# Seven products of halves in eight couples of the up product, and another order of the last token blocks

## The chip, the cores and the metric

The kernel runs on one core of a Trainium2 chip. The metric is device time in microseconds (us) of one execution; lower is better. A core has TensorE (PE in the profile; PEld is its weight load), VectorE (DVE), ScalarE (ACT), GpSimd (POOL) and SyncE (SP, which here only issues loads). Matmuls write to PSUM, eight banks of 128 x 512 float32; DVE and ACT read PSUM, POOL does not. All data are float32.

## The reference

One encoder layer over 512 tokens of width 1024:

```python
h = _rmsnorm(x, g_pre_mix)
q, k, v, g, u, sv, a_ret, a_sgu = jnp.split(h @ w_in, ...)
y_ret = _retention_branch(q, k, v, g, ret_decay_logit, w_ret_o)
y_sgu = _sgu_branch(u, sv, sgu_ln_g, sgu_ln_b, w_spatial, b_spatial, w_sgu_o)
merged = sigmoid(a_ret) * y_ret + sigmoid(a_sgu) * y_sgu
x = x + _rmsnorm(merged @ w_out, g_post_mix)
h2 = _rmsnorm(x, g_pre_ffn)
hid = h2 @ w_up                      # 1024 -> 2 * 2816
hid = conv over 3 neighbouring tokens, per channel, + conv_b
a, b = jnp.split(hid, 2, axis=-1)
x = x + _rmsnorm((gelu(a) * b) @ w_down, g_post_ffn)
```

The change concerns `h2 @ w_up` and the last few microseconds after `@ w_down`.

## The kernel before

Every matrix product is made in three matmuls: each operand is split into a high part (`hi`, rounded to the matmul's type by an ACT copy) and a low part (`lo = src - hi`, by DVE), and hi·hi, hi·lo and lo·hi are accumulated (`split` L80 to L82; `copy` L75 is the ACT copy). Activations are split once, weights as they arrive.

Weights come as 146 blocks of 128 x 1024 in the order of their use (`wall`). The list `units` (L88 to L107) says what each block becomes: `("blk", i)` is a block split whole (`w_block`); a pair of blocks can also become seven forms, `B11, B21, T1, T2, T3, T4, B22` (`w_form`, L143): the four quarters and their sums T1 to T4, each of 512 columns with its own ACT copy and DVE low. T1 and T3 are DVE adds (L154, L155), T2 and T4 POOL adds (L156, L158). `w_get` hands out the next unit and emits the loads and splits of the units ahead of it, up to nine half-size slots (`w4`); raw blocks have four buffers.

Products of seven: a two-by-two block product is made from seven products of halves in place of eight (Strassen's scheme in Winograd's form). The class `Pair` (L637) does it for two output tiles: `part1` makes four products, `part2` one, `part3` two; each product is 4 k-steps x 3 matmuls of 256 columns (L651), in three PSUM banks, with combinations on DVE and ACT between them. For this it needs sums of activation halves, S1 to S4, that `x_forms` (L280) makes on DVE with ACT copies. The u product (4 Pairs) and the two gate products (8 Pairs, each with two whole blocks `f_block` between its parts, L744 to L752) use it already. The down product uses a scheme of seven too, in its own functions.

The up product does not. Its 44 output tiles of 128 channels (`NF` = 22 tiles i, each with an a and a b half) are `f_block` calls (L626): 8 k-steps x 3 matmuls of 512 columns (L203 to L205). The first four of the 44 are made in two token halves by `early` (L874) while the norm before is still being finished. Loop L948: for each tile the two results go through `conv` (an ACT activation L906, then two DVE operations that read PSUM, L909 and L913), `gated` (ACT gelu, DVE product into `gp`, L922), and after every second tile, for seven pairs, `down_forms` (L929), which prepares the forms of `gp` for the down product: five DVE operations of 256 columns, three lows of 512, and four ACT copies.

At the end (L1067), after the second half of the down product, each of the four token blocks t has its last matmuls (`add_whole`, L993) into two banks: M2 and M3 for t = 0 and 1, M4 and M8 for t = 2 and 3. DVE adds them up (`z`, L1076), ACT sums the squares, POOL takes the power (L815), DVE scales and adds x1 (L1084), and SP and ACT queues write the output.

Order: the code's order is the priority. A planner places every instruction in its engine's queue at build time, the earliest ready one in program order first, by its own estimates; each queue then runs in that fixed order, and waits by semaphores. A PSUM bank is guarded as a whole: a matmul into one half waits for a read of the other half that stands before it.

Of the kernel before, what the change touches and what calls it, by code (L numbers as in the profile page):

```python
# [33 lines left out]
DP = 9  # L34
WHOLE = NF - 2 * DP
EAGER = 7

PRE, FFNG, LNG, LNB = 0, 8, 16, 24
CW, CB = 32, 32 + 3 * 2 * NF
# [4 lines left out]
def tile_block(ctx: ExitStack, tc, xT, x, wall, par, cs, decay, wsp, bsp, gpost, gffn, out):  # L44
# [11 lines left out]
    def blk(dt=F32, n="blk", shape=(P, S)):  # L56
        return sb.tile(list(shape), dt, tag="blk", bufs=NBLK, name=nm(n))

    def tmp(n="tmp", shape=(P, S)):
        return sb.tile(list(shape), F32, tag="tmp", bufs=6, name=nm(n))  # L60
# [24 lines left out]

    RES1 = NW - 22 - 44
    RES0 = RES1 - RES_OUT
    units = []  # L88
    i = 0
    while i < NW:  # L90
        pair = [(f, i) for f in ("B11", "B21", "T1", "T2", "T3", "T4", "B22")]
        if U0 <= i < GATE0:
            units += pair
            i += 2
        elif GATE0 <= i < GATE1:
            units += pair[:4] + [("blk", i + 2)] + pair[4:] + [("blk", i + 3)]
            i += 4
        elif i == DOWN0:
            for _ in range(2):
                pairs = [[("q", i + j), ("t", i + j)] for j in range(DP)]  # L100
                whole = [[("blk", i + DP)], [("blk", i + DP + 1)]]
                for u in pairs[:4] + whole[:1] + pairs[4:6] + whole[1:] + pairs[6:] if i == DOWN0 else pairs + whole:
                    units += u
                i += DP + WHOLE // 2
        else:
            units.append(("blk", i))
            i += 1  # L107
# [8 lines left out]
    def w_block(i):  # L116
        raw = raw_tile() if i else raw0
        resident = RES0 <= i < RES1
        if i > 0:
            nc.sync.dma_start(raw, wall[i])  # L120
        if resident:
            hi, lo = [], []
            for c in range(2):
                h_, l_ = blk(F32R, "wh"), blk(F32R, "wl")
                split(h_, l_, raw[:, c * S : (c + 1) * S])
                hi.append(h_)
                lo.append(l_)
        else:
            at = 48 if i >= DOWN0 else 0
            hi, lo = slot("wh", at), slot("wl", at)  # L130
            if i == 0:
                pieces = [slice(0, P), slice(P, S), slice(S, 2 * S)]
                for f in pieces:
                    if f.start:
                        nc.sync.dma_start(raw[:, f], wall[i, :, f])
                    (nc.vector.tensor_copy if f.start == 0 else copy)(hi[:, f], raw[:, f])
                for f in pieces:
                    nc.vector.tensor_sub(lo[:, f], raw[:, f], as32(hi[:, f]))
            else:
                split(hi, lo, raw)  # L140
        return hi, lo
# [21 lines left out]
    def w_down(form, i):  # L163

        if form == "q":
            raw = w_raw["q"] = raw_tile()
            nc.sync.dma_start(raw, wall[i])
            raw = raw[:, : 3 * 256]
        else:
            b, raw = w_raw["q"], raw_tile()  # L170
            two = "p (n c) -> p n c"
            nc.vector.tensor_tensor(
                out=raw[:, :512].rearrange(two, n=2), in0=b[:, :512].rearrange(two, n=2),
                in1=b[:, None, 768:].to_broadcast([P, 2, 256]), op=ALU.add,
            )
            nc.vector.tensor_add(raw[:, 512:768], raw[:, :256], b[:, 256:512])
            nc.vector.tensor_add(raw[:, 768:], raw[:, 512:768], b[:, 512:768])
        w = 768 if form == "q" else 1024
        hi, lo = slot("dh", 48, w), slot("dl", 48, w)
        split(hi, lo, raw)  # L180
        return hi, lo

    def w_unit(u):
        return w_block(u[1]) if u[0] == "blk" else w_down(*u) if u[0] in "qt" else w_form(*u)

    def w_size(u):
        return 2 if u[0] in ("blk", "q", "t") else 1
# [89 lines left out]
    T0, T1 = slice(0, 256), slice(256, 512)  # L277
    forms = {n: [] for n in ("S1", "S2", "S3", "S4")}

    def x_forms(k):  # L280

        a, b = xg[k], xg[k + 4]
        s_ = blk(n="xs")
        nc.vector.tensor_sub(s_[:, T0], a[:, T1], b[:, T1])
        nc.vector.tensor_sub(s_[:, T1], s_[:, T0], a[:, T0])
        nc.vector.tensor_sub(a[:, T0], a[:, T0], a[:, T1])
        nc.vector.tensor_add(a[:, T1], b[:, T0], s_[:, T1])
        for names, s_ in (("S1", "S2"), s_), (("S3", "S4"), a):
            h_, l_ = blk(F32R, "sh"), blk(F32R, "sl")
            split(h_, l_, s_)  # L290
            for n, t in zip(names, (T0, T1)):
                forms[n].append((h_[:, t], l_[:, t]))
# [344 lines left out]
    class Pair:  # L637


        def __init__(self, func, alloc):  # L640
            self.func, self.t = func, [alloc(), alloc()]
            self.b = [ps() for _ in range(3)]

        def product(self, b, act, first, w=None):
# [9 lines left out]
                    )  # L654
            return o

        @staticmethod
        def x(first, t):
            return lambda k: (xh[first + k][:, t], xl[first + k][:, t])

        @staticmethod
        def s(n):
            return lambda k: forms[n][k]

        def part1(self):
            c0, c1 = self.t
            o = self.product(0, self.x(0, T0), True)
            copy(c0[:, T0], o)
            o = self.product(1, self.x(4, T0), True)
            v.tensor_add(c0[:, T0], o, c0[:, T0])  # L670
            self.product(2, self.s("S1"), True)
            o = self.product(0, self.s("S2"), False)
            copy(c1[:, T0], o)
            v.tensor_mul(c0[:, T0], c0[:, T0], rbc[:, T0])

        def part2(self):
            c0, c1 = self.t
# [5 lines left out]
        def part3(self):  # L683
            c0, c1 = self.t
            o = self.product(0, self.x(4, T1), False, self.w[0])
            v.tensor_mul(c0[:, T1], o, rbc[:, T1])
            nc.scalar.activation(out=c0, in_=c0, func=self.func)
            o = self.product(2, self.s("S4"), False, self.w[1])
            v.tensor_sub(c1[:, T0], o, c1[:, T0])
            v.tensor_mul(c1, c1, rbc)  # L690
            nc.scalar.activation(out=c1, in_=c1, func=self.func)


    nc.sync.dma_start(wst, wsp)
# [5 lines left out]
    copy(rws, rw)  # L700
    uT, late = [], None
    for j in range(KD // 2):
        p = Pair(AF.Gelu_apprx_tanh, lambda: blk(n="u"))
        p.part1()
        if late:
            late.part3()
        p.part2()
        late = p
        uT += p.t
# [32 lines left out]


    def gated_pair(ah, al, late=None):  # L744
        p = Pair(AF.Sigmoid, lambda: tmp("sig"))
        p.part1()
        if late:
            late.part3()
        o = [f_block(ah, al, KD)]
        p.part2()  # L750
        o.append(f_block(ah, al, KD, p.part3))
        return zip(o, p.t)  # L752
# [65 lines left out]

    gpm = bcast(gpost, "gpm")
    h2h, h2l = [], []  # L820
    x1 = [[dp_.tile([P, S], F32, tag=f"x1_{t}{n}", name=f"x1_{t}{n}") for n in range(2)] for t in range(NT)]
    for k in range(KD):
        h2h.append(blk(F32R, "h2h"))
# [121 lines left out]
            "S3": (th[:, T0], tl[:, T0]), "S4": (th[:, T1], tl[:, T1]),  # L945
        })

    for i in range(NF):  # L948
        cc = []
        for s_ in range(2):  # L950
            e = 2 * i + s_
            o = early_o[e] if e < EARLY else f_block(h2h, h2l, KD)
            cc.append(conv(o, e))
        gated(*cc)
        if i % 2 and i // 2 < EAGER:
            down_forms(i // 2)

# [104 lines left out]
            first_share(j - 2)  # L1064
    ww = [w_get(), w_get()]
    m[M8] = ps()
    for t in range(NT):  # L1067
        xt = halves("x1")
        for n in range(2):
            nc.sync.dma_start(xt[n], x1[t][n])  # L1070
        for g in range(2):
            add_whole(m, t, g, ww[g], g == 1)
        z, zs_ = tmp("z"), tmp("zs")
        for i, (b, e) in enumerate((((M2, e1), (M3, xx)), ((M4, uu), (M8, yy)))[t // 2]):
            f = slice((t % 2) * 256, (t % 2 + 1) * 256)
            v.tensor_add(z[:, i * 256 : (i + 1) * 256], m[b][:, f], e[:, f])  # L1076
        mean_square(qn[t], 1, z)
        v.tensor_mul(zs_, z, gpf[1])
        sc = row_scale(qn[t])
        zt = (zg[t], zs_)  # L1080
        for i, (a, b) in enumerate(((0, 512), (512, 768), (768, 1024)) if t == NT - 1 else ((0, 512), (512, 1024))):
            f = slice(a % S, a % S + b - a)
            o = zt[a // S][:, f]
            v.scalar_tensor_tensor(  # L1084
                out=o, in0=o, scalar=sc, in1=xt[a // S][:, f], op0=ALU.mult, op1=ALU.add
            )
            (nc.sync, nc.scalar)[i % 2].dma_start(out[t, :, a:b], o)
# [21 lines left out]
def _two(a):  # L1109

    b = _parts(a, 8, P).reshape(4, 2, P, 2, S)
    return np.stack([
        np.concatenate([b[:, 0, :, 0], b[:, 1, :, 0]], -1), np.concatenate([b[:, 1, :, 1], b[:, 0, :, 1]], -1),
    ], 1)


def _gates(a, w):
# [81 lines left out]
```

## Time and profile before

| | us |
|---|---|
| median of 3 runs (841.12 to 846.71) | 841.49 |
| profiled execution | 841.63 |
| its span, first to last instruction | 839.8 |
| PE busy in the span | 827.2 |
| DVE busy | 615.1 |
| ACT busy | 401.5 |
| POOL busy | 76.0 |
| weight blocks of the up product, 501.68 to 719.47 | 217.79 |
| last matmul ends at | 831.3 |

A row of the profile reads: source line, engine, operation, output<-inputs with the program's names, shapes, count, then busy time and mean duration. Rows of the timeline begin with the start in us from the span's start and the length; a bracket gives the idle time of the engine ahead of it and what ended it. `ps` is any PSUM tile, `raw` a weight block as loaded, `wh` and `wl` its parts, `wf` the parts of a form, `cv` a convolved tile.

### The profile page before, as it was taken

How to read it: one execution, taken by the hardware profiler on the slowest of the kernel's cores; microseconds unless marked ns; L12 is line 12 of the kernel's file. 1: busy time of each engine (PE TensorE's matmuls, PEld its weight loads, DVE VectorE, ACT ScalarE, POOL GpSimd, SP SyncE). 2: the span in 40 equal slices, each digit the busy share in tenths (PEclk: the TensorE clock that was granted, in tenths of full speed). 3: DMA queues.
4: the chain of work that ended last, by engine and by line, in shares of the span. 5: the costliest groups of instructions: out<-in, count | busy, mean ns of one | idle time of the engine just before them, and what ended most of it. 6: DMA issues, size and time to landing. Idle time of an engine off the chain costs nothing.

```text
span 839.8 us, 12386 instructions
## 1 busy us (share of the span) xinstructions
PE 827.2 (98%) x4864; PEld 731.3 (87%) x4864; DVE 615.1 (73%) x996; ACT 401.5 (48%) x649; POOL 76.0 (9%) x87
## 2 busy tenths in 40 slices
PE   8999999999999999999999999999999999999995
PEld 6888888888899999999988898888888888999995
DVE  5689898877897776867665767667777556886956
ACT  5635445545664533444444664444444333643531
POOL 0010000102221111132211200000000000000001
PEclk9999999999999999999999999999999999999998
DMA  7733222213233332323457123323222221242532
GB/s 266 265 114 101 76 76 76 75 51 101 87 100 103 101 101 101 101 78 102 149 163 287 66 85 101 101 100 101 97 85 95 100 76 50 80 135 100 159 132 101
DMA packets 29243, 93.19 MB, mean 111 GB/s; under 512 B 3392, under 2 KB 4032, under 8 KB 29184
## 3 DMA queue, kind: packets, MB, share of 16 engines
q1 hardware_dynamic: 26928, 86.85, 31.1%
q0 software_dynamic: 1392, 4.46, 1.5%
q10 hardware_dynamic: 864, 1.09, 0.4%
q8 instruction: 38, 0.62, 0.3%
q14 instruction: 21, 0.17, 0.1%
HBM read 88.19 MB, written 4.19 MB: 110 GB/s over the span
## 4 chain that ended last, share of the span: by engine, by line
PE 96%; DVE 1%; DMA 1%; issue 1%; ACT 0%; POOL 0%; DVEq 0%; SPq 0%; POOLq 0%; ACTq 0%
PE ps L204 16%; PE ps L203 16%; PE ps L205 16%; PE ps L651 14%; PE ps L977 10%; PE ps L465 5%; PE ps L464 5%; PE ps L466 5%; PE ps L798 2%; PE ps L796 2%; PE ps L797 2%; PE ps L993 2%; PE ps L721 1%; DMA raw<-wall 1%; PE ps L264 1%
## 5 line engine op out<-in xcount | busy, mean ns | idle before, releaser
L82 DVE TENSOR_TENSOR wl<-raw,wh 128x1024 fp32r<-128x1024 f32 (+1 forms) x109 | 128.2, 1184 | 100.0 <-PE ps L204 63.7
L205 PE MATMUL ps<-h2h,wl 128*128 128x512 f32 (+1 forms) x384 | 142.3, 371 | 0.0
L204 PE MATMUL ps<-h2l,wh 128*128 128x512 f32 (+1 forms) x384 | 142.2, 371 | 0.0
L203 PE MATMUL ps<-h2h,wh 128*128 128x512 f32 (+1 forms) x384 | 142.2, 372 | 0.0
L75 ACT ACTIVATE wh<-raw 128x1024 fp32r<-128x1024 f32 (+2 forms) x111 | 109.8, 998 | 37.7 <-DMA raw<-wall 18.1
L75 ACT ACTIVATE wf<-raw 128x512 fp32r<-128x512 f32 x84 | 50.8, 627 | 73.5 <-issue 30.2
L203 PEld LDWEIGHTS ps<-h2h,wh 128*128 128x128 f32 x384 | 72.1, 188 | 12.8 <-ACT h2h L863 0.3
L204 PEld LDWEIGHTS ps<-h2l,wh 128*128 128x128 f32 x384 | 72.2, 188 | 12.6
L205 PEld LDWEIGHTS ps<-h2h,wl 128*128 128x128 f32 x384 | 72.2, 188 | 12.3
L82 DVE TENSOR_TENSOR wf<-raw,wf 128x512 fp32r<-128x512 f32 x84 | 65.8, 799 | 19.9 <-ACT wf L75 19.6
L906 ACT ACTIVATE cv<-ps,part 128x512 f32<-128x512 f32 x44 | 34.4, 781 | 87.9 <-PE ps L205 87.9
L464 PE MATMUL ps<-wh,xh 128*128 128x512 f32 x192 | 75.0, 391 | 0.0
L465 PE MATMUL ps<-wl,xh 128*128 128x512 f32 x192 | 74.9, 390 | 0.0
L466 PE MATMUL ps<-wh,xl 128*128 128x512 f32 x192 | 74.8, 390 | 0.0
L651 PE MATMUL ps<-sh,wf 128*128 128x256 f32 x384 | 72.8, 280 | 0.0
L651 PEld LDWEIGHTS ps<-sh,wf 128*128 128x128 f32 x384 | 60.9, 188 | 0.7 <-ACT u L75 0.2
L977 PE MATMUL ps<-dh,fh 128*128 128x256 f32 x216 | 60.3, 279 | 0.0
L977 PE MATMUL ps<-dl,fh 128*128 128x256 f32 x216 | 60.2, 279 | 0.0
L977 PE MATMUL ps<-dh,fl 128*128 128x256 f32 x216 | 60.2, 279 | 0.0
L651 PE MATMUL ps<-xh,wf 128*128 128x256 f32 x288 | 54.6, 281 | 0.0
L651 PE MATMUL ps<-sl,wf 128*128 128x256 f32 x192 | 53.6, 279 | 0.0
L82 DVE TENSOR_TENSOR dl<-raw,dh 128x768 fp32r<-128x768 f32 (+1 forms) x36 | 39.2, 1091 | 18.7 <-PE ps L204 7.9
(290 smaller groups left out, 1851.7 us busy)
## 6 DMA issues: line engine op xcount, KB each, us to landing
raw<-wall SPq DMA_DIRECT2D x145, 512.0 KB, 3.4
x<-x SPq DMA_DIRECT2D x24, 256.0 KB, 5.8
xT<-xT SPq DMA_DIRECT2D x8, 256.0 KB, 5.5
x<-x POOLq DMA_DIRECT2D x8, 256.0 KB, 2.3
xT<-xT POOLq DMA_DIRECT2D x4, 256.0 KB, 3.8
out<-zg SPq DMA_DIRECT2D x4, 256.0 KB, 2.0
out<-zs ACTq DMA_DIRECT2D x3, 256.0 KB, 2.0
cs<-cs SPq DMA_DIRECT2D x2, 256.0 KB, 4.1
```

The costliest lines, as they stand in the source:

```text
L75: nc.scalar.activation(out=o, in_=i, func=AF.Copy)
L82: nc.vector.tensor_sub(lo, src, as32(hi))
L203: nc.tensor.matmul(o, ah, bh, start=start, stop=False)
L204: nc.tensor.matmul(o, ah, bl, start=False, stop=False)
L205: nc.tensor.matmul(o, al, bh, start=False, stop=stop)
L464: nc.tensor.matmul(acc[t], xh[k][:, c], wh[:, f], start=k == 0, stop=False)
L465: nc.tensor.matmul(acc[t], xh[k][:, c], wl[:, f], start=False, stop=False)
L466: nc.tensor.matmul(acc[t], xl[k][:, c], wh[:, f], start=False, stop=k == KD - 1)
L651: nc.tensor.matmul(o, w_[:, c], a_, start=first and k == n == 0, stop=k == 3 and n == 2, skip_group_check=True,)
L796: nc.tensor.matmul(o, ah, bh, start=k == 0, stop=False)
L906: nc.scalar.activation(out=c, in_=o, func=AF.Identity, scale=col(CW + 3 * m + 1), bias=col(CB + m))
L977: nc.tensor.matmul(o, a_[:, c], w_[:, f], start=j == t == i == 0, stop=j == DP - 1 and i == 2 and n not in (M2, M3, M4), skip_group_check= ...
```

## The change

In the up product tiles 3 to 18 are taken as eight couples (3, 4), (5, 6) ... (17, 18). In a couple the first tile's two outputs are made by a `Pair` (seven products of halves), and the second tile's two by whole `f_block`s that stand between the Pair's parts as in the gate stage. `Pair` can now take other activations (`h2h`, `h2l` and forms `h2forms`), and, with no scale given, only combines its products: then its outputs are two SBUF tiles of the `tmp` kind, that `conv` reads in place of PSUM. The weights of a couple's first tile are arranged in quarters on the host (`_up`) and become seven forms.

Ahead of the tiles stand the forms of h2: for each of four k, POOL adds the high and low part of two tiles back together, and `x_forms` makes S1 to S4 from them. `down_forms` is called after tiles 3, 7, 11 and 15, and then after 18, 19 and 20 (before: after every second tile from 1 to 13). The last token blocks are taken as 0, 2, 1, 3.

```diff
+UP0 = DOWN0 - 2 * NF
+COUPLES = [(i, i + 1) for i in range(3, 19, 2)]
...
+        elif i == UP0 + 2 * COUPLES[0][0]:
+            for a, b in COUPLES:
+                pair = [(f, UP0 + 2 * a) for f in FORMS]
+                units += pair[:4] + [("blk", UP0 + 2 * b)] + pair[4:] + [("blk", UP0 + 2 * b + 1)]
+            i = UP0 + 2 * COUPLES[-1][1] + 2
...
-    def x_forms(k):
-
-        a, b = xg[k], xg[k + 4]
+    def x_forms(k, a=None, b=None, forms=forms):
+
+        a, b = a or xg[k], b or xg[k + 4]
...
-        def __init__(self, func, alloc):
-            self.func, self.t = func, [alloc(), alloc()]
+        def __init__(self, func, alloc, a=None, scale=None):
+            self.func, self.t, self.scale = func, [alloc(), alloc()], scale
+            self.h, self.l, self.forms = a or (xh, xl, forms)
...
-            v.tensor_mul(c0[:, T0], c0[:, T0], rbc[:, T0])
+            if self.scale is not None:
+                v.tensor_mul(c0[:, T0], c0[:, T0], self.scale[:, T0])
...
             o = self.product(0, self.x(4, T1), False, self.w[0])
-            v.tensor_mul(c0[:, T1], o, rbc[:, T1])
-            nc.scalar.activation(out=c0, in_=c0, func=self.func)
+            if self.scale is None:
+                copy(c0[:, T1], o)
+            else:
+                v.tensor_mul(c0[:, T1], o, self.scale[:, T1])
+                nc.scalar.activation(out=c0, in_=c0, func=self.func)
             o = self.product(2, self.s("S4"), False, self.w[1])
             v.tensor_sub(c1[:, T0], o, c1[:, T0])
-            v.tensor_mul(c1, c1, rbc)
-            nc.scalar.activation(out=c1, in_=c1, func=self.func)
+            if self.scale is not None:
+                v.tensor_mul(c1, c1, self.scale)
+                nc.scalar.activation(out=c1, in_=c1, func=self.func)
...
-    for i in range(NF):
-        cc = []
-        for s_ in range(2):
-            e = 2 * i + s_
-            o = early_o[e] if e < EARLY else f_block(h2h, h2l, KD)
-            cc.append(conv(o, e))
-        gated(*cc)
-        if i % 2 and i // 2 < EAGER:
-            down_forms(i // 2)
+    def tile_done(i, o):
+        gated(*(conv(t, 2 * i + s_) for s_, t in enumerate(o)))
+        if i < COUPLES[-1][1]:
+            if i % 4 == 3:
+                down_forms(len(dforms))
+        elif len(dforms) < EAGER:
+            down_forms(len(dforms))
+
+    for k in range(4):
+        h2 = halves("h2")
+        for i in range(2):
+            nc.gpsimd.tensor_tensor(out=h2[i], in0=as32(h2h[k + 4 * i]), in1=as32(h2l[k + 4 * i]), op=ALU.add)
+        x_forms(k, *h2, h2forms)
+    couples = dict(COUPLES)
+    i = 0
+    while i < NF:
+        if i in couples:
+            p = Pair(None, lambda: tmp("c"), (h2h, h2l, h2forms))
+            p.part1()
+            o = [f_block(h2h, h2l, KD)]
+            p.part2()
+            o.append(f_block(h2h, h2l, KD, p.part3))
+            tile_done(i, p.t)
+            tile_done(i + 1, o)
+            i += 2
+        else:
+            o = []
+            for e in (2 * i, 2 * i + 1):
+                o.append(early_o[e] if e < EARLY else f_block(h2h, h2l, KD))
+            tile_done(i, o)
+            i += 1
...
-    for t in range(NT):
+    for t in (0, 2, 1, 3):
```

More of the change, by code (lines that the diff above doesn't have):

```diff
@@ L87, in tile_block @@
     RES0 = RES1 - RES_OUT
+    FORMS = ("B11", "B21", "T1", "T2", "T3", "T4", "B22")
     units = []
@@ L90, in tile_block @@
     while i < NW:
-        pair = [(f, i) for f in ("B11", "B21", "T1", "T2", "T3", "T4", "B22")]
+        pair = [(f, i) for f in FORMS]
         if U0 <= i < GATE0:
@@ L183, in w_unit @@
     def w_unit(u):
-        return w_block(u[1]) if u[0] == "blk" else w_down(*u) if u[0] in "qt" else w_form(*u)
+        return w_block(u[1]) if u[0] == "blk" else (w_down if u[0] in "qt" else w_form)(*u)
     def w_size(u):
@@ L655, in product, with x, s @@
             return o
[L657 to L663, printed above, removed]
+        def x(self, first, t):
+            return lambda k: (self.h[first + k][:, t], self.l[first + k][:, t])
+        def s(self, n):
+            return lambda k: self.forms[n][k]
         def part1(self):
@@ L702, in tile_block @@
     for j in range(KD // 2):
-        p = Pair(AF.Gelu_apprx_tanh, lambda: blk(n="u"))
+        p = Pair(AF.Gelu_apprx_tanh, lambda: blk(n="u"), None, rbc)
         p.part1()
@@ L744, in gated_pair @@
     def gated_pair(ah, al, late=None):
-        p = Pair(AF.Sigmoid, lambda: tmp("sig"))
+        p = Pair(AF.Sigmoid, lambda: tmp("sig"), None, rbc)
         p.part1()
@@ L820, in tile_block @@
     h2h, h2l = [], []
+    h2forms = {n: [] for n in ("S1", "S2", "S3", "S4")}
     x1 = [[dp_.tile([P, S], F32, tag=f"x1_{t}{n}", name=f"x1_{t}{n}") for n in range(2)] for t in range(NT)]
@@ L1114, in _two, with _up @@
     ], 1)
+def _up(a):
+    for i, _ in COUPLES:
+        b, c = a[2 * i].reshape(P, 2, S), a[2 * i + 1].reshape(P, 2, S)
+        a[2 * i : 2 * i + 2] = np.stack([
+            np.concatenate([b[:, 0], c[:, 0]], -1), np.concatenate([c[:, 1], b[:, 1]], -1),
+        ])
+    return a
 def _gates(a, w):
@@ L1166 @@
         _rows(i["w_out"]),
-        _inter(_parts(up[:, :DFF], NF, P), _parts(up[:, DFF:], NF, P)),
+        _up(_inter(_parts(up[:, :DFF], NF, P), _parts(up[:, DFF:], NF, P))),
         _down(i["w_down"]),
```

## The prediction

> **What bounds the kernel now.** I read the page first (busy shares, then the chain that ended last), then the windows and the by-shape groups of the stage that is changed, then its timeline by engine.
>
> ```profile
> span 839.8 us, 12386 instructions
> PE 827.2 (98%) x4864; PEld 731.3 (87%) x4864; DVE 615.1 (73%) x996; ACT 401.5 (48%) x649; POOL 76.0 (9%) x87
> PE 96%; DVE 1%; DMA 1%; issue 1%; ACT 0%; POOL 0%; DVEq 0%; SPq 0%; POOLq 0%; ACTq 0%
> ```
>
> The chain is TensorE (PE) nearly from end to end, so a matmul taken out is worth its spacing, as long as VectorE (DVE) keeps feeding it. The windows show how near that is. Columns: stretch, length, then busy time of PE, PEld, DVE, ACT, POOL with counts, clock, DMA share, GB/s.
>
> ```profile
> 501.68:719.47 217.79, 217.79 (x964) 180.35 (x963) 147.36 (x209) 97.00 (x130) 0.00 (x0) 1.00 0.28 92
> 224.88:263.14 38.26, 38.26 (x333) 38.11 (x334) 33.85 (x53) 24.31 (x45) 9.09 (x7) 1.00 0.37 124
> 380.01:400.87 20.86, 20.86 (x135) 18.93 (x134) 15.31 (x21) 9.34 (x17) 5.93 (x4) 1.00 0.30 102
> 545.00:566.81 21.81, 21.81 (x98) 18.06 (x97) 15.32 (x22) 10.27 (x14) 0.00 (x0) 1.00 0.28 96
> 650.00:671.80 21.80, 21.80 (x98) 18.06 (x97) 11.97 (x15) 8.22 (x11) 0.00 (x0) 1.00 0.29 97
> ```
>
> First row: the 40 whole weight blocks of the up product, 217.79 / 40 = 5.445 us each, no PE idle. Second: the u products, halves only; VectorE is busy 33.85 of 38.26 us (88%) and PE still never waits. Third: one step of the gate stage, seven products of halves and two whole blocks, the very mixture that the change makes: 20.86 us. Fourth and fifth: two tiles of the up stage now, 21.8 us, VectorE busy 15.32 us where they hold one `down_forms`, 11.97 where none, so 3.35 for one.
>
> **The change: TensorE.** A couple takes 20.86 in place of 21.81 us: 0.95 each, and 8 couples make -7.6 us. The bounds come from products of 12 matmuls:
>
> ```profile
> 389.75 5.66 PE ps L651 x48
> 224.88 38.26 PE ps L651 x332
> ```
>
> The first gives 0.118 us a matmul and is between blocks as in the couples; the second 0.115. By it a couple takes 84 x 0.115 + 2 x 5.445 = 20.55, and eight save 10.1. I take 7.6, from the nearer row. "TensorE: Matmul & The Clock Gate" of the Trainium skill (Back-to-back issue gap) puts a warm matmul at N / 2.4 ns plus about 2.5: 215.8 ns for 512 columns, 109.2 for 256. By it a couple saves 48 x 0.2158 - 84 x 0.1092 = 1.19 us, eight 9.5, and the sum below would be 1.9 us lower. The trace has both shapes some 5 to 8% slower than the rule, and the measurement decides.
>
> **VectorE in the couples.** What one instruction takes of VectorE, start to start, and what the lock with GpSimd (POOL) does:
>
> ```profile
> 613.85 0.42 DVE L82 TENSOR_TENSOR fa<-gp,fa 128x256 fp32r<-128x256 f32 x1
> 614.19 0.42 DVE L935 TENSOR_TENSOR fs<-gp,gp 128x256 f32<-128x256 f32 x1
> ...
> 616.86 1.22 DVE L82 TENSOR_TENSOR wl<-raw,wh 128x1024 fp32r<-128x1024 f32 x1
> 617.99 0.75 DVE L909 SCALAR_TENSOR_TENSOR cv<-ps,part,cv 128x511 f32<-128x511 f32 x1
> 618.65 0.69 DVE L82 TENSOR_TENSOR fl<-gp,fh 128x512 fp32r<-128x512 f32 x1
> 619.25 0.75 DVE L913 SCALAR_TENSOR_TENSOR cv<-ps,part,cv 128x511 f32<-128x511 f32 x1
> ```
> ```profile
> 228.91 1.78 POOL L156 TENSOR_TENSOR raw<-raw,raw 128x512 f32<-128x512 f32 x1 [3.94 <-DMA raw<-wall]
> 229.45 1.78 DVE L82 TENSOR_TENSOR wf<-raw,wf 128x512 fp32r<-128x512 f32 x1
> 389.58 3.01 POOL L766 TENSOR_TENSOR sig<-sig,r 128x512 f32<-128x512 f32 x2 [6.38 <-DVE sig L765]
> 389.85 0.69 DVE L765 TENSOR_TENSOR sig<-ps,sig 128x512 f32<-128x512 f32 x1 [0.35 <-PE ps L205]
> ```
> ```profile
> L82 DVE TENSOR_TENSOR wf<-raw,wf 128x512 fp32r<-128x512 f32 x84 | 65.8, 799 | 19.9 <-ACT wf L75 19.6
> L155 DVE TENSOR_TENSOR raw<-raw,raw 128x512 f32<-128x512 f32 x12 | 11.6, 964 | 0.7 <-DMA raw<-wall 0.7
> L158 POOL TENSOR_TENSOR raw<-raw,raw 128x512 f32<-128x512 f32 x12 | 15.9, 1322 | 63.6 <-DVE wf L82 63.6
> ```
>
> Prices: 0.34 us for 256 columns, 0.60 for 512, 1.13 for 1024, 0.66 for half a convolution. The 0.69 us form takes 1.78 beside a POOL add, 1.1 more, because both read two SBUF tiles; one that reads PSUM (389.85) isn't slowed. A couple adds on VectorE seven form lows (4.2), the sums T1 and T3 (1.2) and three combinations of 256 columns (1.0), and drops two block lows (-2.3): +4.1. The lock costs by the group means (799 and 964 ns against 690) 7 x 0.11 + 0.27 = 1.0. So 11.97 + 5.1 = 17.1 us in a couple without `down_forms` and 20.4 in one with (now every second one): 18.8 of 20.86 on average, 90%. ScalarE (ACT) gains five small copies net and four evictions: 8 to 10 of 21 us becomes about 13, covered. The weight bytes are the same; loads hold their four raw buffers as in the gate stage (DMA 0.30 beside 0.28). GpSimd has two adds of about 1.3 us a couple, hidden.
>
> The u row shows 88% without a wait, so 90% may just pass. If VectorE could be used to no more than 88%, and each of the two POOL adds cost its full 1.1, the couple would be (17.1 - 1.0 + 2.2 + 3.35 / 2) / 0.885 = 22.6 us: +1.7 each, 14 in all. Bounds 0 to 14; I take 1.5, near the low end, since the u row is nearest and every second couple has 3.7 us to spare. A convolution that is late holds a PSUM bank and one of six temporaries; the next Pair's first copy needs such a temporary 4 us into the couple, so that much lag is free.
>
> **The forms of h2, once.** Ahead of the couples stand eight POOL adds and four times `x_forms`: four 256-column steps, two 512-column lows and two ScalarE copies each.
>
> ```profile
> 490.04 3.15 DVE L866 SCALAR_TENSOR_TENSOR h2l<-ps,part,h2h 128x128 fp32r<-128x128 f32 x8 [3.94 <-ACT h2h L863]
> 494.69 1.22 DVE L82 TENSOR_TENSOR wl<-raw,wh 128x1024 fp32r<-128x1024 f32 x1 [1.49 <-PE ps L204]
> ...
> 515.27 0.69 DVE L922 TENSOR_TENSOR gp<-cv,cv 128x512 f32<-128x512 f32 x1
> 518.06 1.23 DVE L82 TENSOR_TENSOR wl<-raw,wh 128x1024 fp32r<-128x1024 f32 x1 [2.10 <-PE ps L204]
> ```
> ```profile
> 501.68 0.40 PE L203 MATMUL ps<-h2h,wh 128*128 128x512 f32 x1
> ```
>
> h2 is complete at 493.2. PE reaches the first product that needs a form (S1) after blocks 4 and 5 and two products: 501.68 + 2 x 5.445 + 2 x 1.415 = 515.4, 22.2 us later. In just that stretch VectorE is already full (494.69 to 516). It would have to do: the forms of h2 4 x (4 x 0.34 + 2 x 0.60) = 10.2; the lows of blocks 4 and 5, 2.3; four form lows 2.4; T1 and T3 1.2; the convolutions of tiles 0 and 1, 5.3, and their products 1.2; and the lock, 1.1 for each of seven POOL adds (two of the eight run beside 490.04's rows, which read PSUM; one more belongs to T2) 7.7. Together 30.3, 8.1 too much. The moved `down_forms` is already left out. Where the convolutions, which read PSUM, run beside the POOL adds, and T3 and the two products come later, 22.6 is left: 0.4. Bounds 0.4 to 8.1; I take 4, about the middle, because the forms stand ahead of the convolutions in program order but wait for POOL, so some convolutions will slip in between. ScalarE's eight added copies (about 5 us) lie beside this.
>
> **The order 0, 2, 1, 3.**
>
> ```profile
> 826.73 0.28 PE L993 MATMUL ps<-wh,fl 128*128 128x256 f32 x1
> 827.50 0.38 PE L993 MATMUL ps<-wh,fh 128*128 128x256 f32 x1 [0.49 <-DVE z L1076]
> ...
> 828.87 0.28 PE L993 MATMUL ps<-wh,fl 128*128 128x256 f32 x1
> 829.63 0.39 PE L993 MATMUL ps<-wh,fh 128*128 128x256 f32 x1 [0.49 <-DVE z L1076]
> ...
> 831.00 0.28 PE L993 MATMUL ps<-wh,fl 128*128 128x256 f32 x1
> ```
> ```profile
> 832.70 0.42 DVE L1076 TENSOR_TENSOR z<-ps,yy 128x256 f32<-128x256 f32 x1
> ```
> ```profile
> 798.19 0.37 SPq L1070 DMA_DIRECT2D x<-x  x1
> ```
>
> Block 3 shares its two banks with block 2 and waits twice for block 2's reads: steps of 0.77 and 0.76 us in place of 0.115, 1.3 us. With block 1 between them both waits go. But the end is set by VectorE: block 3's last half of `z` starts at 832.70, though PE was done at 831.3, because the two outputs of the block before it stand ahead in the queue. What is late next is that queue. If the order stays, nothing is gained; if `z` follows PE directly (830.0), 2.7. A loss needs late x1 loads, and SP issues the last of them at 798.19, over 20 us before the first block's outputs. Bounds 0 to 2.7; I take 1.0, nearer to no gain, as a third block's `z` meets the same queue.
>
> **Sum.** The profiled execution took 841.63 us (span 839.8); the median of three runs is 841.49, 0.14 less. 841.63 - 7.6 + 1.5 + 4 - 1.0 = 838.5.
>
> **The rivals.** (B) VectorE covers everything: the start costs 0.4, the couples nothing, the end gains its 2.7: 841.63 - 7.6 + 0.4 - 2.7 = 831.7 (829 with products of 0.115). For it: no PE idle at 88%. Against it: a start that is full already. (C) VectorE becomes the bound of the couples, 22.6 us each, slower than the two tiles that they replace: 841.63 - 7.6 + 14 + 4 - 1.0 = 851.0. It decides from 21.81 us of VectorE time and gaps per couple. For it: couples with `down_forms` ask 20.4 of 20.86. Against it: the couples without, and the u row. That PE isn't relieved at all would need products slower than in the gate stage, for which no row speaks.
>
> ```profile
> 826.00:832.00 6.00, 4.29 (x33) 3.69 (x31) 4.87 (x11) 1.45 (x4) 1.10 (x2) 1.00 0.39 151
> 832.00:840.00 8.00, 0.00 (x0) 0.00 (x0) 3.51 (x8) 0.72 (x2) 0.55 (x1) 0.68 0.35 131
> ```
>
> A wait of several us on PE in one piece could also lower the clock: here the granted clock falls (1.00 to 0.68) only after PE has stopped. The Trainium skill ("TensorE: Matmul & The Clock Gate", The HAM clock gate) has half rate after an idle window of about 3.4 us and as long again to recover; by it a start wait in one piece would cost some 1.7 us more, an estimate from the page. No run here shows such a wait, and I count none.
>
> **How the numbers follow.** The forecast has 0.60, B 0.27, C 0.13. 838.5 is the likeliest case; 831 to 848 holds it with B and leaves out most of C and the edge of B. One per cent is 8.4 us, about what a measurement of this kernel tells from no change: below 833.1 lies most of B (0.22), above 849.9 a part of C (0.08), the rest, 0.70, between.
>
> **What would show it.** Couples of 20.9 us on PE, L651 in the up stage at 0.118 us; POOL adds from about 490.5 with DVE rows stretched beside them; PE waiting some 4 us in all between 507 and 520, on forms or weights from DVE; in the couples DVE busy near 90%, PE idle of tenths; no wait of L993 for `z`, and a last `z` at most 2.7 us earlier behind PE. Wrong if couples run at 22 us or more (C), if PE never waits (B), or if the start wait passes 8 us.

## The result, and the profile after

The changed kernel takes 850.43 us (median of 15 runs, 847.39 to 853.11) beside 845.16 for the kernel before (15 runs on the same chip, 840.87 to 846.71): a ratio of 1.0073, 95% interval 1.0054 to 1.0092. It is slower, by less than one per cent; the prediction had it 0.4% faster, and 850.4 lies above its range.

The first lines of the page of the kernel after, and the shares of its chain that ended last:

```profile
span 845.6 us, 13221 instructions
PE 823.7 (97%) x5152; PEld 741.4 (88%) x5152; DVE 662.9 (78%) x1100; ACT 429.7 (51%) x729; POOL 112.4 (13%) x111
PE 91%; DVE 5%; issue 1%; DMA 1%; POOL 1%; ACT 1%; DVEq 0%; SPq 0%; POOLq 0%; ACTq 0%
```

PE's busy time fell by only 3.5 us, though products were taken out, and it has 22 us without work in place of 13. The profiled execution took 847.39 us, against 841.63 before, so 5.8 us are to be found. Stages are cut at three instructions: the first matmul of h2, the first of the down product, and the first of the four last blocks. The times between them, read from PE's timeline of every kernel of this study (e1 to e12 are the experiments below):

| us | start to h2 | h2 to down | down product | last blocks to the end |
|---|---|---|---|---|
| before | 476.6 | 242.68 | 99.06 | 21.43 |
| after | 476.3 | 246.13 | 99.73 | 23.45 |
| e1 after, old order | 481.5 | 245.92 | 101.21 | 21.56 |
| e2 before, new order | 481.3 | 242.68 | 99.21 | 23.43 |
| e3 after, room at the end | 480.5 | 246.43 | 101.13 | 21.09 |
| e4 after, additions on DVE | 481.0 | 243.76 | 99.66 | 23.08 |
| e5 after, Pair tiles in blocks | 481.5 | 251.08 | 101.24 | 23.28 |
| e6 seven couples from 5 | 478.9 | 240.39 | 99.52 | 23.11 |
| e7 e6, three edits | 481.4 | 248.04 | 99.80 | 21.02 |
| e8 e7 with eight couples | 476.2 | 248.34 | 109.32 | 21.04 |
| e9 e6, room at the end | 480.0 | 240.62 | 99.65 | 21.07 |
| e10 e9, forms reversed | 480.9 | 245.85 | 101.51 | 21.13 |
| e11 e9, additions on DVE | 476.6 | 238.28 | 99.85 | 21.17 |
| e12 e11, eight couples from 4 | 480.5 | 239.15 | 99.63 | 21.30 |

The first column holds no stage that an edit changes, and it goes from 476.2 to 481.5: that spread from execution to execution is larger than most effects here, so the other columns are compared, and the timed ratios for the whole. The down product shows a second level too, 101.1 to 101.5 in e1, e3, e5 and e10 with no edit of its own. In these four its matmuls of 256 columns start 0.118 us apart to the end; in the others the spacing falls to 0.113 us, from about 60 us into it on (in e8 and e12 from about 30 us on), and the granted clock is 1.00 in both (read in the kernel before and in e1). What sets the spacing was not found.

Between before and after the columns give -0.3, +3.45, +0.67 and +2.02. The windows of the kernel after say where PE stood (columns as in the prediction): two couples, the stretches around two waits, and the last tiles ahead of the down product.

```profile
549.46:570.32 20.86, 20.86 (x135) 18.93 (x133) 19.86 (x30) 11.83 (x20) 2.94 (x2) 1.00 0.31 101
570.32:591.17 20.85, 20.85 (x134) 18.92 (x133) 16.04 (x28) 12.62 (x22) 2.94 (x2) 1.00 0.32 102
...
494.48:498.00 3.52, 3.52 (x17) 3.52 (x18) 3.52 (x6) 1.24 (x3) 3.52 (x3) 0.55 0.02 5
525.50:529.00 3.50, 3.44 (x14) 3.35 (x15) 3.50 (x6) 2.04 (x6) 0.00 (x0) 0.51 0.31 97
690.00:722.00 32.00, 32.00 (x143) 26.50 (x142) 32.00 (x56) 18.18 (x29) 0.00 (x0) 1.00 0.15 50
```

The couples run as forecast, 20.86 us each with PE never idle. In the third and fourth row the granted clock (the number behind POOL's) is about a half. PE's waits in that stage, by who was waited for, with the total, the count and the longest:

```profile
PE ps L661 <- ACT c L77: 3.5, 1, 3.5
PE ps L212 <- DVE h2l L880: 2.1, 1, 2.1
PE ps L661 <- ACT sh L77: 0.7, 1, 0.7
PE ps L661 <- DVE sl L84: 0.3, 1, 0.3
```

All lie between 492 and 526, at the start. (Lines have moved: products of seven L661, `f_block` L211 to L213, lows L84, copies L77, `z` L1112.) The kernel after, DVE's timeline at the first wait:

```profile
492.70 1.47 DVE L292 TENSOR_TENSOR xs<-h,h 128x256 f32<-128x256 f32 x1 [1.42 <-POOL h L973]
494.08 0.60 DVE L880 SCALAR_TENSOR_TENSOR h2l<-ps,part,h2h 128x128 fp32r<-128x128 f32 x2
494.61 0.98 DVE L293 TENSOR_TENSOR xs<-xs,h 128x256 f32<-128x256 f32 x1
495.50 0.60 DVE L880 SCALAR_TENSOR_TENSOR h2l<-ps,part,h2h 128x128 fp32r<-128x128 f32 x2
```

DVE idles 1.42 us for POOL's additions, then runs the first step of `x_forms` (L292), and only behind it makes the pieces of h2l that PE is waiting for. The step that would take 0.42 takes 1.47, beside POOL's additions. PE stands until 494.48. The third wait and the longest one, in ACT's timeline and then in POOL's and DVE's:

```profile
519.65 0.63 ACT L77 ACTIVATE wf<-raw 128x512 fp32r<-128x512 f32 x1 [2.73 <-POOL raw L164]
520.19 0.61 ACT L77 ACTIVATE sh<-xs 128x512 fp32r<-128x512 f32 x1
...
525.12 0.38 ACT L77 ACTIVATE c<-ps 128x256 f32<-128x256 f32 x1 [2.18 <-DVE gp L936]
```
```profile
490.13 11.15 POOL L973 TENSOR_TENSOR h<-h2h,h2l 128x512 f32<-128x512 f32 x8 [7.37 <-DVE h2l L880]
516.33 3.29 POOL L164 TENSOR_TENSOR raw<-raw,raw 128x512 f32<-128x512 f32 x1 [15.05 <-DVE raw L162]
```
```profile
516.18 0.41 DVE L292 TENSOR_TENSOR xs<-h,h 128x256 f32<-128x256 f32 x1
516.51 0.68 DVE L163 TENSOR_TENSOR raw<-raw,raw 128x512 f32<-128x512 f32 x1
517.12 0.41 DVE L293 TENSOR_TENSOR xs<-xs,h 128x256 f32<-128x256 f32 x1
517.45 0.68 DVE L84 TENSOR_TENSOR wf<-raw,wf 128x512 fp32r<-128x512 f32 x1
...
524.35 1.28 DVE L936 TENSOR_TENSOR gp<-cv,cv 128x512 f32<-128x512 f32 x2
```

One addition on POOL (T2, L164) takes 3.29 us while DVE runs two-input work without a break. The line of this addition, with the least, the median and the longest of its twenty in ns:

```profile
L164 POOL TENSOR_TENSOR raw<-raw,raw x20: 1288/1658/3290, 188.2 to 658.1; 128x512 f32<-128x512 f32 x20
```

ACT stands for it, with the high part of the sum that PE needs (`sh`) queued behind. Then the Pair's first copy `c` waits 2.18 us for a temporary: the six are full until DVE has multiplied the late convolutions of the first tiles (L936).

Added up, the start took 3.45 + 8 x 0.95 = 11.0 us more: 6.6 of waits, and 3.5 x 0.45 + 3.5 x 0.49 = 3.3 by the slow clock behind two of them, which leaves 1.1. By place, from PE's timeline: the stretch from the first matmul of h2 to the first whole block took 28.90 us in place of 25.05, and the first couple 27.72 where the others take 20.86, together 10.7. The other 0.3 is that four whole blocks take 21.76 us from start to start (501.68 to 719.31 is 217.63 us for 40), not 21.81, so that eight couples gave 7.2 us and not 7.6.

At the end no row of PE waits for `z` any more, but ACT's queue shows this:

```profile
829.18 0.35 ACTq L1123 DMA_DIRECT2D out<-zs  x1
831.60 0.63 ACT L820 ACTIVATE junk<-z 128x512 f32<-128x512 f32 x1 [5.34 <-DMA out<-zs]
```

and the chain that ended last runs through that transfer:

```profile
829.18 2.03 DMA out<-zs
```

The second block's square waits until the first block's output has left. The new order keeps `e1` and `xx` alive until the third block; with `uu` and `yy` they hold four of six temporaries. `zs` of the first block, until it has left, and `z` of the second block hold the other two, and the square needs one more for its own output `junk`. Which tiles hold them is read from the code and from the order of the rows; e3 below tests the cause.

### The profile page after: what moved, and what is told of

It is laid out like the page before. It is cut to its first block, busy times and chain, and to the rows that moved or that the text cites. A ratio compares the mean times of both kernels' runs of the same rounds, so it can differ in the third digit from the quotient of the medians.

```text
span 845.6 us, 13221 instructions
## 1 busy us (share of the span) xinstructions
PE 823.7 (97%) x5152; PEld 741.4 (88%) x5152; DVE 662.9 (78%) x1100; ACT 429.7 (51%) x729; POOL 112.4 (13%) x111
## 4 chain that ended last, share of the span: by engine, by line
PE 91%; DVE 5%; issue 1%; DMA 1%; POOL 1%; ACT 1%; DVEq 0%; SPq 0%; POOLq 0%; ACTq 0%
PE ps L661 23%; PE ps L211 11%; PE ps L212 11%; PE ps L213 11%; PE ps L1013 10%; PE ps L472 5%; PE ps L473 5%; PE ps L474 5%; PE ps L809 2%; PE ps L811 2%; PE ps L810 2%; PE ps L1029 2%; PE ps L734 1%; DMA raw<-wall 1%; PE ps L272 1%
## 5 line engine op out<-in xcount | busy, mean ns | idle before, releaser
L84 DVE TENSOR_TENSOR wl<-raw,wh 128x1024 fp32r<-128x1024 f32 (+1 forms) x93 | 108.8, 1180 | 55.4 <-PE ps L661 32.8
L77 ACT ACTIVATE wf<-raw 128x512 fp32r<-128x512 f32 x140 | 84.7, 627 | 96.7 <-PE ps L212 41.2
L84 DVE TENSOR_TENSOR wf<-raw,wf 128x512 fp32r<-128x512 f32 x140 | 107.2, 782 | 26.7 <-ACT wf L77 26.1
L661 PE MATMUL ps<-sh,wf 128*128 128x256 f32 x640 | 123.4, 282 | 4.2 <-ACT c L77 3.5
L77 ACT ACTIVATE wh<-raw 128x1024 fp32r<-128x1024 f32 (+2 forms) x95 | 93.1, 989 | 41.8 <-DMA raw<-wall 19.5
L661 PEld LDWEIGHTS ps<-sh,wf 128*128 128x128 f32 x640 | 102.6, 189 | 5.4 <-ACT c L77 3.7
L212 PE MATMUL ps<-h2l,wh 128*128 128x512 f32 (+1 forms) x256 | 93.7, 367 | 2.1 <-DVE h2l L880 2.1
L211 PE MATMUL ps<-h2h,wh 128*128 128x512 f32 (+1 forms) x256 | 93.8, 369 | 0.0
L213 PE MATMUL ps<-h2h,wl 128*128 128x512 f32 (+1 forms) x256 | 93.3, 365 | 0.0
L661 PE MATMUL ps<-sl,wf 128*128 128x256 f32 x320 | 90.2, 282 | 0.3 <-DVE sl L84 0.3
L164 POOL TENSOR_TENSOR raw<-raw,raw 128x512 f32<-128x512 f32 x20 | 36.2, 1811 | 221.5 <-DVE raw L162 175.9
L661 PEld LDWEIGHTS ps<-sl,wf 128*128 128x128 f32 x320 | 61.6, 193 | 1.1 <-DVE sl L84 0.5
L213 PEld LDWEIGHTS ps<-h2h,wl 128*128 128x128 f32 x256 | 49.2, 192 | 7.8
L211 PEld LDWEIGHTS ps<-h2h,wh 128*128 128x128 f32 x256 | 49.0, 192 | 7.2 <-ACT h2h L877 0.3
L661 PE MATMUL ps<-xh,wf 128*128 128x256 f32 x288 | 54.5, 281 | 0.0
```

What stands on the lines that cost most here:

```text
L77: nc.scalar.activation(out=o, in_=i, func=AF.Copy)
L84: nc.vector.tensor_sub(lo, src, as32(hi))
L164: nc.gpsimd.tensor_tensor(out=w_raw["T2"], in0=w_raw["T1"], in1=w_raw["B22"], op=ALU.add)
L211: nc.tensor.matmul(o, ah, bh, start=start, stop=False)
L212: nc.tensor.matmul(o, ah, bl, start=False, stop=False)
L213: nc.tensor.matmul(o, al, bh, start=False, stop=stop)
```

## The experiments

Each kernel was timed beside the kernel before. Edits are shown against the kernel after, unless said.

**The order.** e1 takes the old order back; e2 is the kernel before with the new order alone; e3 gives the end four tiles from another pool (`blk`, the buffers that the stages before have freed).

```diff
-    for t in (0, 2, 1, 3):
+    for t in range(NT):                                   # e1
...
-    e1, uu, xx, yy = tmp("e1"), tmp("uu"), tmp("xx"), tmp("yy")
+    e1, uu, xx, yy = blk(n="e1"), blk(n="uu"), blk(n="xx"), blk(n="yy")   # e3
```

> The changed kernel with the token blocks of the end taken as 0, 1, 2, 3 again. In the changed profile the end, from the first matmul of the last blocks (822.31) to the last instruction (845.6), takes 23.3 us, before it took 21.3 (818.53 to 839.8). Theory: the new order itself costs these 2.0 us, because the temporaries e1 and xx stay in use until the third block, so that the second block's ACT square waits (5.34 us idle at 831.60, ended by the DMA out<-zs of the first block) for a temporary. Then the end takes 21.3 us again and the kernel is 2.0 us faster than the changed one, about 3.7 us slower than before. Rival 1: the end is longer because of what the couples leave behind (a later start of the DVE queue), not the order: then it stays at 23.3. Rival 2, my prediction's: the new order gains 1.0: then the end gets longer still, 24 or more.

> The kernel before with nothing changed but the order of the last token blocks, 0, 2, 1, 3. Theory (the temporaries): 2.0 us slower than before, 843.6 where the profile of before has 841.6, with the second block's square on ACT waiting for the DMA out<-zs of the first block. Rival (the prediction): 1.0 us faster, bounds 0 to 2.7.

> The changed kernel, but the four tiles of the second half of the down product (e1, uu, xx, yy) come from the large pool blk in place of the six temporaries, so that the last token blocks have all six. Theory: no square waits for an output DMA, PE doesn't wait for z either, and the end takes 18.6 to 21.3 us in place of 23.3, so 2.0 to 4.7 us off the changed kernel. Rival (the new order is bad for another reason, such as the DVE queue's order): the end stays above 22.5 us.

Measured: e1 850.87 us, ratio 1.0067 (1.0043 to 1.0091); e2 848.29, 1.0033 (1.0010 to 1.0056); e3 849.30, 1.0048 (1.0022 to 1.0074). The ratios of e1 and e3 can't be told from that of the kernel after, since 2 us are 0.24%. The last column of the table can: 21.56, 23.43 and 21.09 beside 23.45 after and 21.43 before. So the order costs 2.0 us, in either kernel, as the theory of e1 and e2 said, and all of it is the temporaries. With room the end is 0.3 shorter than before, not the 1.0 of the forecast; the old order with room was not run, so that these 0.3 belong to order and room together. ACT's timeline of e3 has the second square wait for its own block's work in DVE:

```profile
835.21 0.63 ACT L820 ACTIVATE junk<-z 128x512 f32<-128x512 f32 x1 [2.98 <-DVE z L1112]
```

**POOL beside VectorE.** e4 makes the eight sums on DVE.

```diff
-            nc.gpsimd.tensor_tensor(out=h2[i], in0=as32(h2h[k + 4 * i]), in1=as32(h2l[k + 4 * i]), op=ALU.add)
+            nc.vector.tensor_tensor(out=h2[i], in0=as32(h2h[k + 4 * i]), in1=as32(h2l[k + 4 * i]), op=ALU.add)
```

> The changed kernel with the eight adds h2h + h2l on VectorE in place of GpSimd. In the changed profile PE waits 2.1 us at 494.48 for the last pieces of h2l, which stand on DVE behind the first x_forms step, that takes 1.47 in place of 0.42 us beside a POOL add; then the granted clock is 0.50 to 0.60 until 498, 1.75 us more. The up stage, from the first h2 matmul (489.7) to the first matmul of the down product (722.6), takes 232.9 us. Theory A (the lock with GpSimd is what jams the start): without it the wait at 494 and its slow clock go, and the later jam shrinks by 8 x 1.1 - 8 x 0.6 = 4 us: the up stage takes 225 to 229 us. Theory B (the sheer amount of VectorE work is what jams it, whoever holds the lock): 4.8 us of VectorE work are added, and the up stage takes 232 us or more.

Measured: 849.81 us, ratio 1.0047 (1.0023 to 1.0070); h2 to down 243.76, 2.4 less than after. Its waits and POOL's timeline:

```profile
PE ps L661 <- DVE sl L84: 1.8, 1, 1.8
PE ps L661 <- ACT c L77: 1.4, 1, 1.4
PE ps L661 <- ACT wf L77: 0.9, 1, 0.9
```
```profile
518.98 3.23 POOL L164 TENSOR_TENSOR raw<-raw,raw 128x512 f32<-128x512 f32 x1 [31.50 <-DVE raw L162]
```

The wait for h2l is gone, so POOL's additions made it: in the kernel after DVE stood 1.42 us for them and lost 1.05 beside them (1.47 for 0.42) ahead of the piece that PE waits 2.09 for. The jam at the first Pair stays, spread over other partners; the T2 addition still takes 3.23 us. The result lies between the two theories, which speaks for two causes, of which this edit removes one.

**The six temporaries at the first Pair.** e5 takes the Pair's tiles from `blk`.

```diff
-            p = Pair(None, lambda: tmp("c"), (h2h, h2l, h2forms))
+            p = Pair(None, lambda: blk(n="c"), (h2h, h2l, h2forms))
```

> The changed kernel, but the two output tiles of a couple's Pair come from the large pool blk in place of the six temporaries. In the changed profile PE waits 3.47 us at 525.55 for the ACT copy of the first product; ACT sat idle 2.18 us for the DVE product gp, whose convolved tiles are temporaries, and then the granted clock is 0.51 until 529. Theory A (the temporary is what is late): the wait and its slow clock go and the up stage, from the first h2 matmul after the last transposes to the first matmul of the down product, takes 227.5 us in place of 232.9. Theory B (VectorE's backlog is what is late, and the next form or bank is late in its place): it takes 230.5 us or more.

Measured: 856.78 us, ratio 1.0125 (1.0098 to 1.0153); h2 to down 251.08, 5 us worse. Its waits:

```profile
PE ps L213 <- DVE wl L84: 3.6, 1, 3.6
PE ps L661 <- ACT c L77: 2.2, 3, 0.7
PE ps L212 <- DVE h2l L880: 2.1, 1, 2.1
```

The 3.5 us wait for `c` is gone and PE waits 3.6 for block weights instead: DVE was behind with the weights too, as the second theory had it, and the temporaries were only where it showed first. Three waits of 0.7 for `c` in later couples are new. PE's own order is another one there: the Pair's first stretch in a couple has 36 matmuls in place of 48. Why that order is worse was not taken apart.

**Time for the forms.** e6 takes seven couples from tile 5 on, so that two more whole tiles stand between h2 and the first Pair. DVE's work is nearly the same, only due 21.8 us later.

```diff
-COUPLES = [(i, i + 1) for i in range(3, 19, 2)]
+COUPLES = [(i, i + 1) for i in range(5, 19, 2)]
```

> The changed kernel with seven couples, (5, 6) to (17, 18): the first form of h2 is needed 21.8 us later, everything else stands where it stood. Theory A (a jam of the start alone: the couples themselves are covered by VectorE): the waits at 520 to 525.5 go with their slow clock (7.0 us), the wait at 494 with its slow clock (4.0) stays, and one couple less costs 0.95: up stage 232.9 - 7.0 + 0.95 = 226.9 us. Theory B (the couples' VectorE work adds up to a backlog that always ends in a wait): 230 us or more.

Measured: 845.10 us, ratio 0.9986 (0.9968 to 1.0005); h2 to down 240.39, 5.7 less than after and 2.3 less than before. All waits of PE in that stage:

```profile
PE ps L212 <- DVE h2l L880: 2.3, 2, 2.1
PE ps L661 <- ACT c L77: 1.0, 1, 1.0
```

One couple fewer costs 0.95, and still 5.7 us come back, near the 6.0 of the first theory: the jam at the first Pair was a matter of its date. The parts are not all as that theory had them. The wait for h2l stayed, but no slow clock came behind it (the last section), and a wait of 1.0 for `c` in the first couple was left.

**Three edits at once, and apart.** e7 is e6 with the forms of h2 made in the order 3, 2, 1, 0 (the first then needs the last piece of h2l and can't stand ahead of it), and with the Pair's tiles and the end's in `blk`; e8 is e7 with eight couples, 5 to 20. e10 is e7 with the Pair's tiles as before; e9 is e6 with room at the end alone.

```diff
-    for k in range(4):
+    for k in (3, 2, 1, 0):
...
         x_forms(k, *h2, h2forms)
+    for n in h2forms:
+        h2forms[n].reverse()
```

> Seven couples from tile 5; the forms of h2 made in the order k = 3, 2, 1, 0, so that their first step can't stand ahead of the last pieces of h2l; the Pair's tiles and e1, uu, xx, yy of the end in the pool blk. Theory A: no wait of PE at the start at all and the end with all six temporaries: up stage 229.3 (before) - 7 x 0.95 = 222.6 us, end 21.1 us as with the blk tiles alone, so some 7 us faster than before. Theory B (the lock with GpSimd delays the last pieces of h2l or the early weights wherever the adds stand): a wait of 1 to 2 us near 494 and a slow clock stay, up stage 224 to 226.5 us.

> As the kernel with seven couples from tile 5, forms in the order 3, 2, 1, 0 and more room for temporaries, but eight couples, (5, 6) to (19, 20). Theory A: one couple more is worth 0.95 us: up stage 221.7 us. Theory B (the large pool is full at tile 19, when forms of h2 and of gp are both alive, and three down_forms come at once just ahead of the down product): waits of PE near the start of the down product, up and down stage together no shorter than with seven.

> The changed kernel with seven couples, the first at tile 5, and with the four tiles that the end keeps (e1, uu, xx, yy) taken from the block buffers in place of the six temporaries. Theory A (the costs are two separate ones: the forms of h2 when the first couple stands at tile 3, and the temporaries at the end): the stretch from the first product of h2 to the first down product stays at 240.4 us, the stretch from the first of the last blocks to the end at 21.1, the down product at 99.5, so the kernel lies 2.3 + 0.3 = 2.6 us under the kernel before, 842.5 or a ratio of 0.997. Theory B (the buffers taken from the blocks are missed by the block weights' other users, or the end's gain is lost to something late): the end stays over 22 us or the down product grows, and the ratio is 0.999 or more.

> The run before it, with the forms of h2 made in the order 3, 2, 1, 0, so that the first of them needs the last pieces of h2l and can't stand ahead of them in VectorE's queue. Theory A (the wait for h2l at 494 us and the slow clock behind it, 2.1 + 1.75 us, are the rest of the start's cost): the wait goes and nothing takes its place, the stretch from the first product of h2 to the first down product is 240.4 - 4 = 236.4 us. Theory B (the reversed order was what put VectorE's and ScalarE's work ahead of the block weights in the run with all three edits together, and not the place of the couples' copies): a wait of about 7 us for block weights stands near 512 us, and the stretch is 244 to 248 us.

Measured: e7 848.63 us, ratio 1.0043 (1.0025 to 1.0061); e8 857.26, 1.0139 (1.0111 to 1.0167); e9 844.33, 0.9977 (0.9958 to 0.9996); e10 848.41, 1.0025 (1.0010 to 1.0040). The only wait of e10 in the up stage, and the largest of e8 from there to the last blocks:

```profile
PE ps L213 <- DVE wl L84: 7.4, 1, 7.4
```
```profile
PE ps L213 <- DVE wl L84: 7.4, 1, 7.4
PE ps L1015 <- ACT dh L77: 3.9, 3, 2.0
PE ps L1015 <- DVE e L1049: 2.4, 1, 2.4
```

The reversed order takes the wait for h2l away and sets a wait of 7.4 us for block weights in its place, with or without the Pair's tiles; so e10's second theory holds, and neither theory of e7 does. DVE's timeline of e10 shows how: it stands 2.27 us for POOL's additions, runs form steps and convolutions, the first of them stretched, and reaches the low part that PE has waited for since 512 only at 518.15.

```profile
499.75 1.50 DVE L292 TENSOR_TENSOR xs<-h,h 128x256 f32<-128x256 f32 x1 [2.27 <-POOL h L973]
...
518.15 1.21 DVE L84 TENSOR_TENSOR wl<-raw,wh 128x1024 fp32r<-128x1024 f32 x1
```

Between e10 and e7 only the Pair's tiles differ: 245.85 and 248.04, so `blk` costs 2.2 us there too. e8 adds waits in the down product (109.3 us), as its second theory said: its last couple ends two tiles later, and the last three `down_forms` stand just ahead of their use. e9 is what its first theory said, 240.6 and 21.1.

**Both remedies.** e11 is e9 with the eight sums on DVE; e12 is e11 with eight couples, from tile 4.

```diff
-COUPLES = [(i, i + 1) for i in range(3, 19, 2)]
+COUPLES = [(i, i + 1) for i in range(4, 20, 2)]      # e12; e11: range(5, 19, 2)
```

> The run with seven couples from tile 5 and room at the end, with the eight additions that make h2 on VectorE in place of GpSimd. Theory A (GpSimd's additions, which stretch VectorE's two-input subtractions beside them from 0.4 to 1.5 us, are what makes the last pieces of h2l late): the wait for h2l falls under 0.5 us, the granted clock stays up, and the stretch from the first product of h2 to the first down product is 236 to 238 us. Theory B (VectorE has no room: eight additions of about 0.6 us each push the block weights or the forms back): another wait of 1 us or more takes its place, and the stretch is 240 us or more.

> All eight couples, the first one tile later than in the changed kernel (tiles 4 and 5, 6 and 7, to 18 and 19), with the additions on VectorE and room at the end as in the run before it, whose stretch from the first product of h2 to the first down product was 238.3 us with seven couples from tile 5. Theory A (one tile more of whole products, 21.8 us of PE, is enough for the forms of h2): the eighth couple brings its 0.95 us, the stretch is 237.3 us, the down product 99.5 to 100 and the end 21.1; about 5 us under the kernel before. Theory B (the forms need the two tiles, or the down product's own forms, now one tile later, come late): the stretch is 240 us or more, or the down product is over 101 with waits on dh, dl or e.

Measured: e11 840.10 us, ratio 0.9936 (0.9912 to 0.9961); e12 842.42, 0.9957 (0.9937 to 0.9977). e11's only wait in the up stage, DVE's timeline at the place where h2l was late, and e12's waits:

```profile
PE ps L211 <- ACT wh L77: 1.4, 1, 1.4
```
```profile
491.64 0.69 DVE L973 TENSOR_TENSOR h<-h2h,h2l 128x512 f32<-128x512 f32 x1
492.25 0.60 DVE L880 SCALAR_TENSOR_TENSOR h2l<-ps,part,h2h 128x128 fp32r<-128x128 f32 x2
492.77 0.41 DVE L292 TENSOR_TENSOR xs<-h,h 128x256 f32<-128x256 f32 x1
493.11 0.60 DVE L880 SCALAR_TENSOR_TENSOR h2l<-ps,part,h2h 128x128 fp32r<-128x128 f32 x2
```
```profile
PE ps L211 <- ACT wh L77: 1.4, 1, 1.4
PE ps L661 <- ACT c L77: 1.2, 2, 1.0
```

A sum takes DVE 0.69 us, and the steps of `x_forms` are back at 0.41; the forms still stand between the pieces of h2l, but cost too little to hold PE. h2 to down is 238.28, just above the 236 to 238 of its first theory, with the other wait of over 1 us that the second one named; it is 4.4 us less than before, and e11 beats both kernels: by its stages from h2 on it is 3.9 us faster than before. In e12 the forms have one whole tile more than in the changed kernel, which is 10.9 us and not the 21.8 of its expectation, and the eighth couple doesn't pay: 239.15 lies between its theories, with the wait for `c` back at the first two Pairs. The intervals of e11 and e12 overlap.

## Why the prediction was wrong, step by step

**TensorE in the couples, -7.6: right.** 20.86 us was forecast and measured in every couple but the first; with whole blocks counted from start to start the eight gave 7.2.

**VectorE in the couples, +1.5: nothing.** It was forecast at 20.4 and 17.1 us busy and is at 19.86 and 16.04, with PE never idle: rival B's side of the bounds. Rival C, slower because the couples take 22.6 us, gave nearly the measured time (851.0) by a mechanism that isn't there.

**The start, +4 with bounds 0.4 to 8.1: 11.0 (10.7 by place). This is the step that failed.** The mechanism was partly right: DVE's work ahead of the first Pair was too much for its 22 us, and moving the Pair two tiles later (e6) gives it back. Three things were missing. First, the sum of DVE's work was held against one deadline, S1's; the forms also stand in the queue ahead of the last pieces of h2l, whose deadline is 492: 2.1 us (gone in e4 and e11). Second, lateness was counted only as late forms; it came out as T2's addition on POOL (3.29 for 1.29 us), ScalarE's queue behind it, and a temporary, 4.5 us together. The prediction had seen the temporary inside a couple and called its lag free; at the first Pair the convolutions of the first tiles were still unmade. Third, the clock: it counted none, and two waits brought 3.3 us. From the Trainium skill's rule that it weighed ("TensorE: Matmul & The Clock Gate", The HAM clock gate) it had an estimate of 1.7 us for one wait in one piece, which is about what each of the two cost. The lower bound was also added up wrong: 30.3 - 7.7 is 22.6 already, and with T3 (0.6) and the two products (1.2) later, as the text says, 20.8 is left, less than the 22.2 us there were.

**The order, -1.0 with bounds 0 to 2.7: +2.0, outside them.** The step "a loss needs late x1 loads" looked at the loads and not at what the new order keeps alive: `e1` and `xx` through three blocks in place of two. e3 shows what the order was worth with room, -0.3 at most: the queue of DVE that it named as late next does set the end.

**What was not in the sum:** +0.67 in the down product. Three `down_forms` now stand together, DVE is busy all of 690 to 722 (in the windows above), and the group of the down product on the profile's page has waits that it had not before:

```profile
L1013 PE MATMUL ps<-dh,fh 128*128 128x256 f32 x216 | 60.4, 280 | 0.4 <-DVE yy L1048 0.2
```

That is 0.4 us; the rest is no more than the spread of that column. No run shows whether these waits come of the `down_forms`.

The measured sum is -7.6 + 0 + 11.0 + 2.0 + 0.7 - 0.3 = 5.8; the last term is the stretch ahead of h2, which no edit changes.

## What to carry to other kernels

Work that is done once, ahead of a repeated gain, is priced by the deadlines of all that stands behind it in its queue, not by its sum against its own deadline. When a loop's order is changed, list what now lives longer and count the buffers of its pool, output transfers included: two edits here, each with a sound reason, lost 13 us to a jam at the start and a pool of six. If a saving is certain and its preparation is late, start it later: one couple given up, the sums moved off the engine that slowed its neighbour, and buffers for the end turned +0.7% into -0.6%.

## What the runs showed of the hardware

The same wait of 2.09 us for h2l is followed by a slow clock in one kernel and not in another. The 3.52 us behind it, in e6 and then in e9:

```profile
497.07:500.59 3.52, 3.35 (x25) 3.15 (x26) 3.52 (x6) 1.24 (x3) 3.52 (x3) 1.00 0.02 5
```
```profile
498.15:501.67 3.52, 3.35 (x18) 3.15 (x19) 3.52 (x6) 1.24 (x3) 3.52 (x3) 0.69 0.02 5
```

1.00 in e6, 0.69 in e9, and 0.55 in the kernel after; the times of DVE, ACT and POOL agree, and PE issues fewer matmuls where the clock is lower. The mean hides when the slow stretch begins. Cut at its edges, in the kernel after and then in e9:

```profile
494.80:498.21 3.41, 3.41 (x18) 3.41 (x17) 3.41 (x5) 0.92 (x3) 3.41 (x4) 0.50 0.02 5
```
```profile
499.51:502.93 3.42, 3.36 (x15) 3.36 (x16) 3.42 (x5) 0.41 (x1) 3.42 (x3) 0.50 0.02 5
```

Both are half clock for 3.4 us; the first begins 0.3 us after the end of the wait, the second 1.4 us after it. The same wait (2.09 or 2.10 us) stands in e1, e3 and e5 too, and there 3.41 or 3.42 us at 0.50 begin 0.1 us before its end, 1.0 and 0.6 us after it. So the clock behind this wait cost half of 3.4, about 1.7 us, in five kernels and nothing in one. At the waits of 3.6 us in e5 and 7.4 in e7 and e10 the clock is at 0.50 for 6.82 to 6.84 us, twice as long, a part of it still inside the wait. Waits of 1.0 to 1.4 us in e6, e11 and e12 were followed by no slow clock; in e4 one of 1.84 and one of 1.39 us, a microsecond apart, were.

The Trainium skill ("TensorE: Matmul & The Clock Gate", The HAM clock gate) has an activity window of about 3.4 us that runs freely. That would explain that the outcome depends on when the wait falls, and the trace agrees that the slow stretch lasts 3.4 us or twice that. It also speaks of an idle window of about 3.4 us before the clock falls; here 2.09 us without work were enough, less than that. No run here moved the same wait in small steps, so the bound stays open.

GpSimd and VectorE slowed each other more here than in the rows of the kernel before, where a form of 0.69 us took 1.78 beside an addition on POOL: 256-column steps of DVE went from 0.42 to as much as 1.51 us (498.62 in the kernel after), and one 512-column addition of POOL from 1.29, the least of its line, to 3.29 us beside a run of two-input operations.
